# An encoder block on one core: separate banks for the first two block products of the feed-forward part, scratch tiles taken out, loads moved into the down projection, rotary tables computed earlier

## The chip, the cores and the metric

The kernel runs on one core of a Trainium2 chip. The metric is device time in microseconds (us) of one execution. Before the change three timed runs took 2662.81, 2665.69 and 2669.3 us, a median of 2665.69. The engines of the core are TensorE (PE, the matrix multiplies), VectorE (DVE), ScalarE (ACT), GpSimd (POOL) and SyncE (SP, which issues most of the DMAs, in order). PE writes into PSUM, which here is used as 8 banks of 128 partitions by 512 floats. Everything else is held in SBUF tiles.

## The reference

One sequence of S = 1024 tokens of width D = 1024 goes through DEPTH = 2 layers, all in f32:

```python
h = rms_norm(x, norm_mix_g[i])
z = h @ w_in[i]
q = apply_partial_rope(rms_norm(q, q_norm_g[i]), cos, sin)      # and k
o_attn = windowed_gqa_with_sink(q, k, v, sink[i])               # +-128 tokens
uv = gelu(z[..., GM_OFF:CONV_OFF]); o_gm = spatial_gating(uv, ...)
o_conv = conformer_conv(z[..., CONV_OFF:IN_COLS], ...)          # GLU, 31 taps, norm, swish
merged = concat(rms_norm(o_attn), rms_norm(o_gm), rms_norm(o_conv))
x = x + merged @ w_out[i]
hf = rms_norm(x, norm_ffn_g[i]) @ w_gate_up[i]                  # D_FF = 2816, gate and up
x = x + (silu(hf[..., :D_FF]) * hf[..., D_FF:]) @ w_down[i]
gate = sigmoid(rms_norm(x, ple_norm_g[i]) @ w_ple_gate[i])
x = x + (p[i] @ w_ple_proj[i]) * gate
```

## The kernel before

Activations are kept with features on the partitions and tokens along the row, in two halves of 512 tokens. Every product of two f32 operands is made of three matmuls in a reduced format: each operand is cut into a high part, which ACT copies out (`copy_h`, L122), and a low part, which DVE (sometimes POOL) gets by subtraction (`sub_l`, L125; for whole weight tiles L216). `step_mm` (L222 to L229) issues wh·hi (L224), wh·lo (L226) and wl·hi (L228) of 512 columns each.

A layer runs in stages. First come the input projection and the mixers. The 30 conv taps per channel block are DVE instructions (L493), issued piece by piece in the background of other work; `setup_gen`, another generator, computes the sine and cosine tables of the rotary step on DVE and ACT (L377 to L417). Then come the output projection (`wo_first`, `wo_second`), the feed-forward part, `down` and `ple`.

The feed-forward part multiplies by blocks, as Strassen's method does, with 7 block products per pair of output tiles where 8 would be the plain way. There are 11 pairs j. `first(j)` makes the two block products that need only the first token half: for gate (i = 0) and up (i = 1), 24 matmuls each, of which the first 12 (k below 4, one product) are read out by DVE as `s1` (L1131), sent to DRAM (`sum_d`), and the other 12 are then added on top in the same bank, so that PE waits at the middle of each unit until DVE has read. `token_forms(k)` makes the token-side sums for the other five products: per k 4 scalings (L1153), a difference `t1` (L1163), another on DVE (L1165), two on POOL, and five splits (L122 and L125). `rest(j)` makes the five other products: for i = 0 and then i = 1 it loads `s1` and two weight tiles `rw` (L1181), forms four weight sums on POOL (L1216, L1218, L1219, L1220; the first into a scratch tile `ws`), splits five weight blocks on ACT and DVE, runs five products of 12 matmuls, and adds and multiplies on DVE (L1208 and silu on ACT L1209 for i = 0; L1212 and L1213, through a scratch tile `cu`, for i = 1). The results go to DRAM (`act_d`, L1233 and L1234).

Order: firsts 0 to 4 run ahead, among the output projection; then the token forms; firsts 5 to 7; then rest 0, first 8, rest 1, first 9, rest 2, first 10, and rests 3 to 10 with nothing between them. After that come the transposes of `p` (L1267), the `ple` weights (L1275), and `down`: for each token half, 22 steps fi, each with a weight tile (`load_w`, L211 to L216), an activation tile `ac` (L1291) that is split, and 24 matmuls into all 8 banks.

Tiles come from pools: 38 `U` tiles of 128 by 1024, 6 `T` tiles of 128 by 512 (`s1`, `ws`, `cu`, `u2`, `g`, `ac`, `sg`, `sq`), 3 buffers each for `raw`, `wh`, `wl`, and PSUM banks `pa` (3), `pt` (4), `po` (1). An allocation waits until the tile that last had the buffer has been used for the last time. A scheduler orders each engine's instructions from the program text and the pools; the engines then run in that order.

Of the kernel before, what the change touches and what calls it, by code (L numbers as in the profile page):

```python
# [8 lines left out]
F32 = mybir.dt.float32  # L9
# [6 lines left out]
P = 128  # L16
# [55 lines left out]
def tile_encoder_trunk(ctx: ExitStack, tc: tile.TileContext, x, p, positions, norm_mix_g, w_in,  # L72
# [368 lines left out]
    for k in range(NK):  # L441
        if k + 1 < NK:
            x_in(k + 1)
        if k >= 3:
            next(setup, None)
# [15 lines left out]
    for layer in range(DEPTH):  # L461
# [656 lines left out]
        def first(j):  # L1118
# [3 lines left out]
            a = None  # L1122
            for i, off in enumerate((0, DFF)):
                wh, wl = load_w(rows_of(w_gate_up[layer], 0, NK, off + c0, P), (NK, P),
                                nc.gpsimd if ahead else None, nc.vector if ahead else None)
                b = BA()
                for k in range(NK):
                    step_mm(b, (wh[:, k, :], wl[:, k, :]), hl0[k], k == 0, k % HK == HK - 1, True)
                    if k == HK - 1:
                        s1 = T("s1")  # L1130
                        nc.vector.tensor_tensor(out=s1, in0=b, in1=bc, op=ALU.mult)  # L1131
                        nc.sync.dma_start(out=sum_d[j][i], in_=s1)
                    if k % 2 == 1:
# [39 lines left out]
        def rest(j):  # L1173

            ga, gb = U("ga"), U("gb")
            for i, off in enumerate((0, DFF)):
# [8 lines left out]
                sm = T("ws")  # L1185
                s3 = sm.rearrange("p (k m) -> p k m", k=HK)
# [19 lines left out]
                def out_of(dst, src, b):  # L1206
# [10 lines left out]
                w22 = None  # L1217
# [10 lines left out]
                out_of(gb[:, 512:1024], g, bc_)  # L1228
# [28 lines left out]

        pT = [[U("pT2", F32R) for _ in range(2)] for _ in range(2)]
        for hf in range(2):
            raw = wp.tile([P, 1024], F32, tag="raw", name=nm("pin"))  # L1260
            r3 = raw.rearrange("p (b m) -> p b m", b=4)
            nc.sync.dma_start(out=r3, in_=p[layer, 0, hf * 512:(hf + 1) * 512, :]
# [125 lines left out]
```

## Time and profile before

| | before |
|---|---|
| median of three timed runs | 2665.69 us |
| profiled execution, its own time | 2667.72 us |
| span of the trace | 2665.9 us |
| mean granted TensorE clock | 0.952 |
| PE busy | 2387.9 us (90%) |
| DVE / ACT / POOL busy | 1453.5 / 905.5 / 744.6 us |
| HBM read and written | 228.84 and 63.96 MB |

The span runs from the first to the last instruction; the profiled execution's own time is 1.8 us longer. [...] Idle time of PE plus the time lost at the lower clock is what an edit that leaves the arithmetic alone can win.

### The profile page before, as it was taken

What the parts mean: (1) busy time and instruction counts of PE and PEld (TensorE: products, weight loads), DVE (VectorE), ACT (ScalarE), POOL (GpSimd) and SP (SyncE); (2) the same over time, 40 slices, a digit from 0 to 9 for tenths busy, and PEclk for the clock granted to TensorE, in tenths of its full rate; (3) what the DMA queues carried; (4) which work ended last, traced back from release to release, by engine and by line L of the source; (5) the groups of instructions that cost most, each with busy time, mean ns of one, the idle gap of its engine ahead of it and who ended that gap; (6) DMA issues with size and microseconds to landing.
All of it is one profiled execution on the core that took longest, in us unless ns stands there. A gap on an engine that the chain in (4) does not pass through costs nothing. (4 is left out here: it accounts for less than half of the span.)

```text
span 2665.9 us, 30234 instructions
## 1 busy us (share of the span) xinstructions
PE 2387.9 (90%) x11404; PEld 1972.8 (74%) x11404; DVE 1453.5 (55%) x2241; ACT 905.5 (34%) x1610; POOL 744.6 (28%) x551
## 2 busy tenths in 40 slices
PE   8898889688988889899999898896898888898999
PEld 6897767567766668688789876675776666786887
DVE  6986674644544452525469567646444444526252
ACT  5246661312222241424323457412212222424142
POOL 5123345532332300103421233464323333001031
PEclk9999998899999989899999999898999999999999
DMA  6011324333333262523321031344333332625332
GB/s 205 24 52 56 119 84 161 118 124 113 131 103 103 87 217 95 198 95 107 96 71 37 33 111 64 126 150 123 123 111 99 103 103 87 241 95 197 95 99 67
DMA packets 243346, 294.78 MB, mean 111 GB/s; under 512 B 11348, under 2 KB 180912, under 8 KB 243200
## 3 DMA queue, kind: packets, MB, share of 16 engines
q1 hardware_dynamic: 236704, 283.16, 32.4%
q10 hardware_dynamic: 6016, 9.45, 1.1%
q8 instruction: 90, 1.47, 0.2%
q0 software_dynamic: 480, 0.24, 0.1%
q14 instruction: 56, 0.46, 0.1%
HBM read 228.84 MB, written 63.96 MB: 110 GB/s over the span
## 5 line engine op out<-in xcount | busy, mean ns | idle before, releaser
L216 DVE TENSOR_TENSOR wl<-raw,wh 128x1024 fp32r<-128x1024 f32 x172 | 218.9, 1273 | 337.5 <-ACT wh L122 327.7
L224 PE MATMUL pt<-tf,wh 128*128 128x512 f32 x792 | 326.5, 415 | 54.7 <-ACT wh L122 54.7
L122 ACT ACTIVATE wh<-raw 128x1024 fp32r<-128x1024 f32 x172 | 182.0, 1059 | 532.2 <-PE pt L226 376.9
L226 PE MATMUL pt<-tf,wh 128*128 128x512 f32 x792 | 323.3, 408 | 0.0
L224 PE MATMUL pa<-hl,wh 128*128 128x512 f32 x648 | 264.4, 409 | 62.9 <-DVE s L1131 52.9
L228 PE MATMUL pt<-tf,wl 128*128 128x512 f32 x792 | 315.4, 404 | 0.0
L224 PE MATMUL pa<-tf,wh 128*128 128x512 f32 x704 | 280.0, 400 | 19.5 <-ACT wh L122 19.5
L264 POOL TENSOR_TENSOR st<-st,sq 128x512 f32<-128x512 f32 x82 | 123.4, 1506 | 610.2 <-ACT sq L263 607.9
L228 PE MATMUL pa<-tf,wl 128*128 128x512 f32 x704 | 273.1, 394 | 9.2 <-DVE wl L125 9.2
L226 PE MATMUL pa<-tf,wh 128*128 128x512 f32 x704 | 277.0, 394 | 0.0
L228 PE MATMUL pa<-hl,wl 128*128 128x512 f32 x648 | 259.1, 404 | 4.5 <-POOL wl L216 3.3
L226 PE MATMUL pa<-hl,wh 128*128 128x512 f32 x648 | 262.1, 405 | 1.0 <-DVE hl L128 0.8
L224 PEld LDWEIGHTS pt<-tf,wh 128*128 128x128 f32 x792 | 159.4, 201 | 98.4 <-ACT wh L122 64.0
L1216 POOL TENSOR_TENSOR ws<-rw,rw 128x512 f32<-128x512 f32 x44 | 63.7, 1448 | 511.5 <-DVE cu L1212 337.6
L224 PEld LDWEIGHTS pa<-hl,wh 128*128 128x128 f32 x648 | 125.8, 194 | 99.6 <-DVE s L1131 59.3
L607 PE MATMUL pa<-wh,hl 128*128 128x256 f32 x640 | 181.1, 288 | 16.4 <-ACT zkv L620 11.7
L226 PEld LDWEIGHTS pt<-tf,wh 128*128 128x128 f32 x792 | 157.6, 199 | 33.9
L228 PEld LDWEIGHTS pt<-tf,wl 128*128 128x128 f32 x792 | 156.3, 197 | 34.2
L609 PE MATMUL pa<-wl,hl 128*128 128x256 f32 x640 | 181.6, 286 | 0.0
L610 PE MATMUL pa<-wh,hl 128*128 128x256 f32 x640 | 180.8, 286 | 0.0
L224 PEld LDWEIGHTS pa<-tf,wh 128*128 128x128 f32 x704 | 134.9, 192 | 55.7 <-ACT wh L122 28.8
L122 ACT ACTIVATE wh<-rw 128x512 fp32r<-128x512 f32 x176 | 102.6, 618 | 208.2 <-POOL rw L1218 172.8
(309 smaller groups left out, 4933.9 us busy)
## 6 DMA issues: line engine op xcount, KB each, us to landing
rw<-in_w_gate_up_dram SPq DMA_DIRECT2D x88, 512.0 KB, 6.0
raw<-in_w_down_dram SPq DMA_DIRECT2D x88, 512.0 KB, 3.6
raw<-in_w_gate_up_dram SPq DMA_DIRECT2D x44, 512.0 KB, 4.5
ac<-act SPq DMA_DIRECT2D x88, 256.0 KB, 5.0
raw<-in_w_ple_gate_dram SPq DMA_DIRECT2D x32, 512.0 KB, 4.1
raw<-in_w_in_dram SPq DMA_DIRECT2D x28, 512.0 KB, 3.8
raw<-in_w_out_dram SPq DMA_DIRECT2D x24, 512.0 KB, 3.7
sum<-s SPq DMA_DIRECT2D x44, 256.0 KB, 2.2
```

Of the source, the lines that this page charges most:

```text
L122: nc.scalar.activation(dst, src, AF.Copy, scale=scale)
L216: (eng or nc.vector).tensor_tensor(out=l, in0=raw, in1=f(h), op=ALU.subtract)
L224: nc.tensor.matmul(b, lhsT=wh, rhs=hl[:, 0:512], start=first, stop=False, skip_group_check=again)
L226: nc.tensor.matmul(b, lhsT=wh, rhs=hl[:, 512:1024], start=False, stop=False, skip_group_check=again)
L228: nc.tensor.matmul(b, lhsT=wl, rhs=hl[:, 0:512], start=False, stop=last, skip_group_check=again)
L264: (eng or nc.gpsimd).tensor_tensor(out=n.s, in0=n.s, in1=sq, op=ALU.add)
L607: nc.tensor.matmul(o, lhsT=x_[:, th], rhs=wh, start=(kc + k == 0), stop=False)
L609: nc.tensor.matmul(o, lhsT=x_[:, th], rhs=wl, start=False, stop=False)
L610: nc.tensor.matmul(o, lhsT=x_[:, tl], rhs=wh, start=False, stop=(kc == 1 and k == 3))
L1216: tt(out=s3, in0=a21, in1=a22, op=ALU.add)
```

## The change

The rotary tables' generator is advanced twice per step from k = 2 on, where it was once from k = 3. `first` loads the weights of both units up front and makes its products in separate banks (the three `pa` for the firsts ahead, `pa` and `pt` in turn for the others): the second bank is scaled in place and `s1` added, so DVE reads or writes a bank 7 times per first where it did 4 times, and the POOL multiply goes. In `rest` the weight sum is written into the left half of `ga`, and the up side adds in place in PSUM. The loads of `p` and of the `ple` weights go into `U` tiles, the `ac` tiles too; the `ple` weights are loaded at fi = 8, and X at fi = 12 of each half.

```diff
@@ -441,8 +441,9 @@
     for k in range(NK):
         if k + 1 < NK:
             x_in(k + 1)
-        if k >= 3:
-            next(setup, None)
+        if k >= 2:
+            for _ in range(2):
+                next(setup, None)
@@ -1119,27 +1120,30 @@
-            a = None
-            for i, off in enumerate((0, DFF)):
-                wh, wl = load_w(rows_of(w_gate_up[layer], 0, NK, off + c0, P), (NK, P),
-                                nc.gpsimd if ahead else None, nc.vector if ahead else None)
-                b = BA()
-                for k in range(NK):
-                    step_mm(b, (wh[:, k, :], wl[:, k, :]), hl0[k], k == 0, k % HK == HK - 1, True)
-                    if k == HK - 1:
-                        s1 = T("s1")
+            ws = [load_w(rows_of(w_gate_up[layer], 0, NK, off + c0, P), (NK, P),
+                         nc.gpsimd if ahead else None, nc.vector if ahead else None)
+                  for off in (0, DFF)]
+            a = T("sg")
+            for i, (wh, wl) in enumerate(ws):
+                bank = BA if ahead else BU
+                s1 = T("s1")
+                for h in range(2):
+                    b = bank()
+                    for k in range(h * HK, (h + 1) * HK):
+                        step_mm(b, (wh[:, k, :], wl[:, k, :]), hl0[k], k % HK == 0,
+                                k % HK == HK - 1)
+                        if k % 2 == 1:
+                            bg.tick()
+                    if h == 0:
                         nc.vector.tensor_tensor(out=s1, in0=b, in1=bc, op=ALU.mult)
                         nc.sync.dma_start(out=sum_d[j][i], in_=s1)
-                    if k % 2 == 1:
-                        bg.tick()
+                    else:
+                        nc.vector.tensor_tensor(out=b, in0=b, in1=bc, op=ALU.mult)
+                        nc.vector.tensor_tensor(out=b if i else a, in0=b, in1=s1, op=ALU.add)
                 if i == 0:
-                    a = T("sg")
-                    nc.vector.tensor_tensor(out=a, in0=b, in1=bc, op=ALU.mult)
                     nc.scalar.activation(a, a, AF.Silu)
-                    nc.gpsimd.tensor_tensor(out=a, in0=a, in1=bc, op=ALU.mult)
-                else:
-                    nc.vector.tensor_tensor(out=a, in0=b, in1=a, op=ALU.mult)
-                    nc.sync.dma_start(out=act_d[2 * j][:, HALF[0]], in_=a)
+            nc.vector.tensor_tensor(out=a, in0=b, in1=a, op=ALU.mult)
+            nc.sync.dma_start(out=act_d[2 * j][:, HALF[0]], in_=a)
@@ -1182,8 +1186,7 @@
-                sm = T("ws")
-                s3 = sm.rearrange("p (k m) -> p k m", k=HK)
+                s3 = ga[:, 0:512].rearrange("p (k m) -> p k m", k=HK)
@@ -1208,13 +1211,11 @@
                     else:
-                        c = T("cu")
-                        nc.vector.tensor_tensor(out=c, in0=b, in1=src, op=ALU.add)
-                        nc.vector.tensor_tensor(out=dst, in0=c, in1=dst, op=ALU.mult)
+                        nc.vector.tensor_tensor(out=b, in0=b, in1=src, op=ALU.add)
+                        nc.vector.tensor_tensor(out=dst, in0=b, in1=dst, op=ALU.mult)
@@ -1225,7 +1226,12 @@
-                out_of(gb[:, 512:1024], g, bc_)
+                if i == 0:
+                    out_of(gb[:, 512:1024], g, bc_)
+                else:
+                    nc.vector.tensor_tensor(out=g, in0=bc_, in1=g, op=ALU.add)
+                    nc.vector.tensor_tensor(out=gb[:, 512:1024], in0=g, in1=gb[:, 512:1024],
+                                            op=ALU.mult)
@@ -1255,44 +1261,50 @@
+        pin = [U("pin").rearrange("p (b m) -> p b m", b=4) for _ in range(2)]
+        for hf in range(2):
+            nc.sync.dma_start(out=pin[hf], in_=p[layer, 0, hf * 512:(hf + 1) * 512, :]
+                              .rearrange("(b q) m -> q b m", q=P))
...
-            raw = wp.tile([P, 1024], F32, tag="raw", name=nm("pin"))
...
-                ps = BT()
+                ps = BU()
...
-            raw = wp.tile([P, 1024], F32, tag="raw", name=nm("praw"))
...
+        def proj_weights():
+            for c in range(2):
+                raw = U("praw")
...
-            xps = [U("X").rearrange("p (m s) -> p m s", m=2) for _ in range(4)]
-            for mp in range(4):
-                nc.sync.dma_start(out=xps[mp], in_=xd[2 * mp:2 * mp + 2, :, HALF[hf]]
-                                  .rearrange("m p s -> p m s"))
             banks = [BO()] + [BA() for _ in range(3)] + [BT() for _ in range(4)]
             for fi in range(NF):
                 wh, wl = load_w(rows_of(w_down[layer], fi * P, 1, 0, D), (1, D))
-                t = T("ac")
+                t = U("ac")[:, 0:512]
...
+                if fi == 8 and hf == 0:
+                    proj_weights()
+                if fi == 12:
+                    xps = [U("X").rearrange("p (m s) -> p m s", m=2) for _ in range(4)]
+                    for mp in range(4):
+                        nc.sync.dma_start(out=xps[mp], in_=xd[2 * mp:2 * mp + 2, :, HALF[hf]]
+                                          .rearrange("m p s -> p m s"))
```

In the rows of the order below, numbers behind a name tell tiles apart.

The order of DVE near the end of the rotary tables in the first layer, before. L493 is a conv tap, `rt` the scratch of the tables; ACT's cosine follows L408:

```order
L383 SCALAR_TENSOR_TENSOR rt_462<-rt_462 128x64
L493 SCALAR_TENSOR_TENSOR acc_715<-glu_684,cols_190,acc_715 128x1019
L383 SCALAR_TENSOR_TENSOR rt_462<-rt_462 128x64
L493 SCALAR_TENSOR_TENSOR acc_715<-glu_684,cols_190,acc_715 128x1020
L383 SCALAR_TENSOR_TENSOR rt_462<-rt_462 128x64
L493 SCALAR_TENSOR_TENSOR acc_715<-glu_684,cols_190,acc_715 128x1021
L377 TENSOR_SCALAR rt_462<-rt_462 128x64
L493 SCALAR_TENSOR_TENSOR acc_715<-glu_684,cols_190,acc_715 128x1022
L408 TENSOR_SCALAR rt_462<-rt_462 128x64
```

And now, where a tap is L494:

```order
L494 SCALAR_TENSOR_TENSOR acc_715<-glu_684,cols_190,acc_715 128x1013
L383 SCALAR_TENSOR_TENSOR rt_388<-rt_388 128x64
L759 TENSOR_TENSOR rot_773<-sinf,qkg 128x8x8 x4
L216 TENSOR_TENSOR wl_1016<-raw_1014,wh_1015 128x1024
L125 TENSOR_TENSOR wst_763<-pt_766,wst_763 128x512
L494 SCALAR_TENSOR_TENSOR acc_715<-glu_684,cols_190,acc_715 128x1014
L377 TENSOR_SCALAR rt_388<-rt_388 128x64
L494 SCALAR_TENSOR_TENSOR acc_715<-glu_684,cols_190,acc_715 128x1015
L408 TENSOR_SCALAR rt_388<-rt_388 128x64
```

L408 stands behind the tap of length 1015 instead of the one of length 1022, that is 7 taps earlier.

The order of POOL in the rests without firsts, before. `ws` is the weight sum, `rw` are the loaded weights; four rows are one unit:

```order
L1216 TENSOR_TENSOR ws_7125<-rw_7121,rw_7122 128x512
L1218 TENSOR_TENSOR rw_7121<-rw_7121 128x4x128
L1219 TENSOR_TENSOR rw_7121<-ws_7125,rw_7121 128x4x128
L1220 TENSOR_TENSOR rw_7122<-rw_7122,rw_7121 128x4x128
L1216 TENSOR_TENSOR ws_7232<-rw_7228,rw_7229 128x512
```

And now, the sum being L1218 into `ga` and the other three L1219 to L1221:

```order
L1220 TENSOR_TENSOR rw_6917<-ga_6814,rw_6917 128x4x128
L1218 TENSOR_TENSOR ga_7016<-rw_7020,rw_7021 128x512
L1221 TENSOR_TENSOR rw_6918<-rw_6918,rw_6917 128x4x128
L1219 TENSOR_TENSOR rw_7020<-rw_7020 128x4x128
L1220 TENSOR_TENSOR rw_7020<-ga_7016,rw_7020 128x4x128
L1221 TENSOR_TENSOR rw_7021<-rw_7021,rw_7020 128x4x128
```

The first sum of the next rest's gate side (`ga_7016`) has moved ahead of the last one of this rest's up side.

The order of SP where `down` begins in the second layer, before. `act_118` and `act_117` are the last results of the feed-forward part, `raw` is a weight tile of `down`:

```order
L1181 DMA rw_16840<-in_w_gate_up_dram 128x4x256
L1275 DMA praw_16984<-in_w_ple_proj_dram 128x1024
L1234 DMA act_118<-gb_16736 128x1024
L1291 DMA ac_17012<-act_97 128x512
L211 DMA raw_17006<-in_w_down_dram 128x1024
L1291 DMA ac_17047<-act_98 128x512
L1291 DMA ac_17082<-act_99 128x512
L1233 DMA act_117<-ga_16735 128x512
```

And now, first a piece in the middle of the rests (`act_102` belongs to rest 2), then the one where `down` begins:

```order
L1185 DMA rw_15309<-in_w_gate_up_dram 128x4x256
L211 DMA raw_16999<-in_w_down_dram 128x1024
L1240 DMA act_102<-gb_15025 128x1024
L211 DMA raw_17034<-in_w_down_dram 128x1024
L1139 DMA sum_0_139<-s_2510_15239 128x512
```

```order
L1185 DMA rw_16822<-in_w_gate_up_dram 128x4x256
L1266 DMA pin_16920<-in_p_dram 128x4x256
L1266 DMA pin_16921<-in_p_dram 128x4x256
L1296 DMA ac_16970<-act_97 128x512
L211 DMA raw_17069<-in_w_down_dram 128x1024
L1296 DMA ac_17005<-act_98 128x512
L1296 DMA ac_17040<-act_99 128x512
L1240 DMA act_118<-gb_16719 128x1024
```

The first three weight tiles of `down` are loaded eight or nine rests earlier; the weight tile that now stands just before the last results is the fourth.

## Rows read from the trace of the kernel before

**Rows 1.** The page's busy line (engine, us, share of the span, instructions), then the view of PE's waits over the whole span: waiting tile and line, what it waited for, us in total, times, longest us.

```profile
PE 2387.9 (90%) x11404; PEld 1972.8 (74%) x11404; DVE 1453.5 (55%) x2241; ACT 905.5 (34%) x1610; POOL 744.6 (28%) x551
...
PE pt L224 <- ACT wh L122: 54.7, 22, 2.5
PE pa L224 <- DVE s L1131: 52.9, 14, 10.9
PE po L224 <- ACT tf L122: 31.1, 4, 8.8
PE pa L224 <- ACT wh L122: 19.5, 22, 0.9
PE pa L607 <- ACT zkv L620: 11.7, 1, 11.7
...
PE pa L228 <- DVE wl L125: 9.2, 14, 0.7
PE pt L511 <- DVE acc L493: 5.8, 1, 5.8
...
PE po L224 <- ACT wh L122: 4.5, 2, 2.3
```

**Rows 2.** The end of the rotary tables in the first layer. Timelines of ACT, DVE and PE (start us, us, engine, line, operation, out<-in, count, idle time before and its releaser), and between them two rows of the view by windows (stretch in us, its length, busy us of PE, PEld, DVE, ACT, POOL with counts, granted clock, DMA share, GB/s).

```profile
91.42 0.26 ACT L410 ACTIVATE cosf<-rt 128x64 f32<-128x64 f32 x1 [17.25 <-DVE rt L408]
...
91.20 0.19 DVE L408 TENSOR_SCALAR rt<-rt 128x64 f32<-128x64 f32 x1
...
92.00:96.00 4.00, 3.91 (x19) 3.91 (x20) 3.96 (x7) 0.76 (x3) 0.00 (x0) 0.53 0.00 0
122.00:192.00 70.00, 70.00 (x588) 70.00 (x587) 64.67 (x87) 29.43 (x58) 14.65 (x7) 1.00 0.15 50
...
189.78 2.57 DVE L493 SCALAR_TENSOR_TENSOR acc<-glu,cols,acc 128x1010 f32<-128x1010 f32 x2
...
195.61 1.58 PE L511 MATMUL pt<-ident,acc 128*128 128x128 f32 x13
```

**Rows 3.** The first of the firsts ahead in the second layer: PE's timeline, and the stretch around it by windows, columns as in rows 2.

```profile
1732.15 0.80 PE L224 MATMUL pa<-hl,wh 128*128 128x512 f32 x1 [1.47 <-DVE s L1131]
...
1738.65 0.50 PE L224 MATMUL pa<-hl,wh 128*128 128x512 f32 x1 [1.01 <-DVE sg L1137]
...
1720.00:1740.00 20.00, 14.20 (x42) 9.91 (x43) 17.53 (x27) 8.13 (x12) 7.22 (x6) 0.66 0.38 133
```

**Rows 4.** Token forms and firsts 5 to 7 in the second layer: the stretch by windows, columns as in rows 2, and rows of DVE's timeline in it.

```profile
1815.00:1870.00 55.00, 32.06 (x109) 23.91 (x108) 43.59 (x52) 17.13 (x30) 24.69 (x15) 0.78 0.29 91
...
1815.73 5.39 DVE L1153 SCALAR_TENSOR_TENSOR X<-X,cols,st 128x512 f32<-128x512 f32 x8 [2.46 <-ACT st L298]
...
1857.19 0.69 DVE L1131 TENSOR_TENSOR s<-pa,st 128x512 f32<-128x512 f32 x1 [2.50 <-PE pa L228]
...
1870.11 1.22 DVE L125 TENSOR_TENSOR wl<-rw,wh 128x512 fp32r<-128x512 f32 x1
```

**Rows 5.** PE's timeline at the middle of first 8's up unit in the second layer, and at the start of the rest behind it.

```profile
1911.56 0.50 PE L224 MATMUL pa<-hl,wh 128*128 128x512 f32 x1 [1.38 <-DVE s L1131]
...
1915.35 0.50 PE L224 MATMUL pa<-tf,wh 128*128 128x512 f32 x1 [0.78 <-ACT wh L122]
```

**Rows 6.** One rest without a first, in the first layer: timelines of PE, DVE and SP where its gate side begins, the time from issue to landing of the `rw` loads (L1181, 8 loads between 850 and 895 us), POOL's timeline for its up side, and the whole period by windows for PE alone (stretch, length, busy us of PE with count, granted clock, DMA share, GB/s).

```profile
855.86 0.50 PE L224 MATMUL pa<-tf,wh 128*128 128x512 f32 x1 [0.94 <-ACT wh L122]
...
854.96 0.69 DVE L1212 TENSOR_TENSOR cu<-pt,u 128x512 f32<-128x512 f32 x1 [0.96 <-PE pt L228]
855.69 1.36 DVE L1213 TENSOR_TENSOR ga<-cu,ga 128x512 f32<-128x512 f32 x1
...
857.08 0.32 SPq L1233 DMA_DIRECT2D act<-ga  x1
...
857.92 2.35 SPq L1181 DMA_DIRECT2D rw<-in_w_gate_up_dram  x4
...
DMA to landing us min/median/max: 4.1/6.0/7.6
...
864.61 1.30 POOL L1216 TENSOR_TENSOR ws<-rw,rw 128x512 f32<-128x512 f32 x1 [8.11 <-DVE g L1226]
...
867.35 1.29 POOL L1219 TENSOR_TENSOR rw<-ws,rw 128x512 f32<-128x512 f32 x1
...
855.00:888.80 33.80, 29.70 (x120) 0.95 0.31 102
```

**Rows 7.** Where `down` begins in the second layer: PE's and SP's timelines, and two stretches by windows, columns as in rows 2.

```profile
2282.64 0.80 PE L224 MATMUL po<-tf,wh 128*128 128x512 f32 x1 [6.85 <-ACT tf L122]
...
2275.83 0.33 SPq L211 DMA_DIRECT2D raw<-in_w_down_dram  x1
...
2282.68 1.97 SPq L211 DMA_DIRECT2D raw<-in_w_down_dram  x3
...
2282.00:2288.00 6.00, 5.36 (x14) 4.24 (x15) 4.27 (x6) 2.90 (x6) 0.00 (x0) 0.58 1.05 398
2294.00:2298.00 4.00, 4.00 (x12) 3.10 (x11) 3.83 (x5) 3.63 (x6) 0.00 (x0) 0.58 1.05 394
```

**Rows 8.** ACT's timeline in the middle of `down` (second layer), where the second token half begins.

```profile
2415.03 0.62 ACT L263 ACTIVATE sq<-X 128x512 f32<-128x512 f32 x1
2416.69 1.92 ACT L122 ACTIVATE tf<-ac 128x512 fp32r<-128x512 f32 x3 [1.05 <-DMA ac<-act]
```

More of the change, by code (lines that the diff above doesn't have):

```diff
@@ L1210, in out_of @@
                     else:
-                        c = T("cu")
-                        nc.vector.tensor_tensor(out=c, in0=b, in1=src, op=ALU.add)
-                        nc.vector.tensor_tensor(out=dst, in0=c, in1=dst, op=ALU.mult)
+                        nc.vector.tensor_tensor(out=b, in0=b, in1=src, op=ALU.add)
+                        nc.vector.tensor_tensor(out=dst, in0=b, in1=dst, op=ALU.mult)
                 bank = BT if i else BA
                 tt(out=s3, in0=a21, in1=a22, op=ALU.add)
-                w22 = None
                 tt(out=a21, in0=a11, in1=a21, op=ALU.subtract)
@@ L1255, in tile_encoder_trunk @@
                 first(AHEAD + 1 + BEHIND + j)
+        pin = [U("pin").rearrange("p (b m) -> p b m", b=4) for _ in range(2)]
+        for hf in range(2):
+            nc.sync.dma_start(out=pin[hf], in_=p[layer, 0, hf * 512:(hf + 1) * 512, :]
+                              .rearrange("(b q) m -> q b m", q=P))
         pT = [[U("pT2", F32R) for _ in range(2)] for _ in range(2)]
         for hf in range(2):
-            raw = wp.tile([P, 1024], F32, tag="raw", name=nm("pin"))
-            r3 = raw.rearrange("p (b m) -> p b m", b=4)
-            nc.sync.dma_start(out=r3, in_=p[layer, 0, hf * 512:(hf + 1) * 512, :]
-                              .rearrange("(b q) m -> q b m", q=P))
             for c in range(2):
-                ps = BT()
+                ps = BU()
                 for b in range(4):
-                    nc.tensor.transpose(ps[:, b * P:(b + 1) * P], r3[:, b, c * P:(c + 1) * P],
+                    nc.tensor.transpose(ps[:, b * P:(b + 1) * P], pin[hf][:, b, c * P:(c + 1) * P],
                                         ident)
@@ L1272, in tile_encoder_trunk @@
         pw = []
-        for c in range(2):
-            raw = wp.tile([P, 1024], F32, tag="raw", name=nm("praw"))
-            nc.sync.dma_start(out=raw, in_=w_ple_proj[layer, c * P:(c + 1) * P, :])
-            ph, pl = U("pwh", F32R), U("pwl", F32R)
-            copy_h(ph, raw)
-            sub_l(pl, raw, ph)
-            pw.append((ph, pl))
+        def proj_weights():
+            for c in range(2):
+                raw = U("praw")
+                nc.sync.dma_start(out=raw, in_=w_ple_proj[layer, c * P:(c + 1) * P, :])
+                ph, pl = U("pwh", F32R), U("pwl", F32R)
+                copy_h(ph, raw)
+                sub_l(pl, raw, ph)
+                pw.append((ph, pl))
         nx = [None, None]
         for hf in range(2):
-            xps = [U("X").rearrange("p (m s) -> p m s", m=2) for _ in range(4)]
-            for mp in range(4):
-                nc.sync.dma_start(out=xps[mp], in_=xd[2 * mp:2 * mp + 2, :, HALF[hf]]
-                                  .rearrange("m p s -> p m s"))
             banks = [BO()] + [BA() for _ in range(3)] + [BT() for _ in range(4)]
```

## The prediction

> **What bounds the kernel now.** I read the page's busy line first, then PE's waits, then the stretches in which they fall. PE is busy 2387.9 us of 2665.9 [rows 1], so TensorE bounds the kernel and 278 us of idle are all that an edit without fewer matmuls can win, apart from what PE loses at the lower clock. The reader is to see in the view of waits that few places make up the large lines, and that the diff touches nearly all of them: 22 waits of about 2.5 us for ACT's weight copy at the up side of a rest, 14 for `s1` (up to 10.9), 4 for a split in `down`, 22 short ones at the gate side of a rest, and one of 11.7 for ACT's `zkv` [rows 1]. Then the timelines tell for each what the engine named was itself waiting for. The sum below is made against the profiled execution's own 2667.7 us (span 2665.9 and 1.8 around it), which lies 2.0 over the median of 2665.7.
>
> **1. Rotary tables.** ACT's cosine stood 17.25 us for DVE's L408, which ended at 91.39, and `zkv` behind it released PE after 11.7 us [rows 1, 2]. In the new order L408 follows 7 taps fewer, at 1.28 us each (two took 2.57) [rows 2]: some 9 us earlier, so the wait shrinks to about 3, and the clock, 0.53 from 92 to 96 [rows 2], costs up to 1.9 less: 9 to 11 us won at this place. But the taps still have to be made. DVE is busy 64.67 us of the 70 from 122 to 192, its last tap ends at 192.35, and PE reads the sum at 195.61 [rows 2]. PE's lead over 3.3 us of slack turns into a wait there, as in the second layer, where PE stood 5.8 us for the taps [rows 1]; what DVE idled (5.3) is the rest that it can make up. I take 4 of bounds -2 and 11, near the slack.
>
> **2. Firsts ahead.** PE stands 1.47 us for `s1` and 1.01 for `sg`, and runs at a mean clock of 0.66 from 1720 to 1740 [rows 3]. The next 12 matmuls now have a bank of their own, and three banks cover the read-out, so both waits go, and the full clock should come about a microsecond sooner. 3.5 a layer, 7 in all, of bounds 0 and 10. More reads of PSUM come with it, 3 per first at 0.69 us [rows 4], on a DVE that is idle there once the token sums have not begun.
>
> **3. Token forms and firsts 5 to 7.** Waits for `s1` add up to 52.9 us [rows 1]; less 1.47 twice and 1.38 eight times (part 4) [rows 3, 5] this stage holds 38.9 of them. From 1815 to 1870 PE is busy 32.06 of 55 us, at a mean clock of 0.78 [rows 4]. It looks like a gain of 20 us a layer. But DVE is busy 43.59 of the 55 [rows 4], and from 1815.73 on its scalings and splits hold the waiting reads back. The separate banks let PE go on until its 7 banks are full; then it waits for the same DVE, which now has 9 reads more for three firsts, 9 x 0.69 = 6.2 us. 43.6 + 6.2 = 49.8 against 55 leaves 5.2 us if DVE never idles, more if part of the reads falls behind the first weights of rest 0, whose low part (L125) is made at 1870.11 [rows 4]. I take 6 a layer, 12 in all, of bounds 0 and 20.
>
> **4. Rests 0 to 3 with firsts between.** Per rest and first PE stands 1.38 us at the middle of the first and 0.78 at the gate side of the rest [rows 5]. The first of these goes with the separate banks, the second with `ws`, whose `T` buffer came free only when DVE had read an older one. 4 x 2.16 x 2 layers = 17.3; I take 17, of bounds 8 (only the first waits go, with something lost) and 18.
>
> **5. Rests alone, 7 a layer.** The period is 33.8 us at a clock of 0.95 [rows 6]. It holds 0.94 and 0.66 (the line of 9.2 over 14) at the gate side and 2.5 at the up side [rows 1, 6], and 1.7 (a twentieth) at the lower clock; the rest, 28.0 for 120 matmuls, makes 0.233 each and 2.8 per product. In the new order POOL makes the next gate side's first sum a unit early, so the gate side's waits go: 1.6 us. What is late next is the up side. Its weights are still loaded behind the store of `ga`: store at 857.08, `rw` from 857.92, POOL's first sum at 864.61 and the third ended at 868.64 [rows 6]. PE left the last product of the rest before at 855.86 - 0.94 = 854.92. Now 4 products (the first has been run ahead) end the gate side at 854.92 + 11.2 = 866.1, not at 870.7. The path through silu holds PE 2.5 us as before, to 868.6. The path through the loads: `ga` took 0.69 + 1.36 on DVE [rows 6] and in place should take 0.69 twice, so the loads, POOL and its third sum come 0.7 us earlier, at 868.0; a copy on ACT of 0.6 leads to 868.6 as well. So two paths meet, and any slip of the loads (4.1 to 7.6 us in this stretch, 6.0 in the middle [rows 6]) is paid in full; the 0.66 for the low part may come back here too. I take 1.0 a rest, 14 in all, of bounds -10 (a slip of 1.6 and a little more low clock in each) and 21 (1.5).
>
> [...]
>
> No row shows DVE writing into PSUM. From both sides: the nearest rows are 0.69 with a PSUM input and 1.36 beside POOL [rows 6]; I take 0.69.
>
> **6. Start of `down`.** SP issued the first weights of `down` at 2275.83, its next at 2282.68 behind the X loads, and PE stood 6.85 us, then about 2.3 [rows 1, 7]. With the first three weight tiles loaded during the rests, the fourth and `ac` on their way before the end, and X out of the queue, I see nothing late behind them. In both layers: the `po` lines hold 31.1 and 4.5 [rows 1]; two of the four long waits are those in the middle of `down`, 8.8 at most each [rows 1], which leaves at least 31.1 - 17.6 + 4.5 = 18. The clock was 0.58 over 6 and 4 us [rows 7]: 4.2 lost a layer, 8.4 in all. 26 of bounds 18 and 28.
>
> **7. Middle of `down`.** ACT ran the second norm's copies and squares until 2415.65, then waited 1.05 us for `ac` [rows 8]. Only that last us can go, since the copies stay ahead of the split: 2 in all, of bounds 0 and 4.
>
> **Sum.** 4 + 7 + 12 + 17 + 14 + 26 + 2 = 82. 2667.7 - 82 = 2585.7, and 2.0 less beside the median: 2584 us.
>
> **Rivals.**
> - DVE decides: the lead at the start is paid back whole, and the token stage gains nothing, since 9 more reads fill the time that PE wins (parts 1 and 3 at 0), and the loads keep the rests at 0.4 us each (6). For it: DVE's 43.59 of 55 and 64.67 of 70 us. Against it: DVE stood 2.50 us for PE at 1857 [rows 4], so it wasn't late all the way. 7 + 17 + 6 + 26 + 2 = 58: 2608. A chance of 0.25.
> - All is had: start 10, token stage 20, rests alone 21. For it: the largest waits have a cause that the diff removes. Against it: DVE's share again. 10 + 8 + 20 + 17 + 21 + 27 + 3 = 106: 2560. 0.15.
> - The loads into `down` don't do what they say: an early weight tile or an `ac` stands behind something unfinished in SP's queue, and the wait moves on to the fourth tile. For it: SP's order is strict. Against it: the three tiles are in place whole rests before. Without the 26: 56, 2610. 0.07.
> - Slower: the up side's loads become the bound of every rest. [...] With 4.5 us more and another 1.7 for 14 rests alone, and 2 for the 8 others, 103 us come in against 82 - 14 = 68 won: 2701. It decides from a slip of about 3 us in all rests. The longest landing, 7.6, is 1.6 over the middle. 0.05.
>
> **How the numbers follow.** The forecast has 0.45 and its own range is 2572 to 2598. What is left, 0.03, is no change, by several of these together. A difference under 0.2% (5 us) can't be told from no change here; faster by more than that 0.92, same 0.03, slower 0.05. The range goes from 2558, which takes in most of the case where all is had, to 2626, over the two at 2608 to 2610 and half of the unknown in part 5.
>
> **What would show it.** In the profile after: `zkv` at about 3 us, and a wait for taps in the first layer too (part 1); no wait for `s1` in the middle of a unit, and PE standing for DVE's reads of a bank in the token stage (3); in a rest alone no wait at the gate side, one of 2.5 to 3.2 at the up side, and a period near 32.8 (5); no wait over a us at the start of `down`, still about 7.5 in its middle (6, 7). The prediction fails if the up side's wait grows past 5 us, if DVE's in-place operations take more than 1 us where POOL is idle, or if the token stage ends no earlier and `down` still starts late.

## The result and the profile after

The changed kernel takes 2594.72 us (median of four, 2591.07 to 2603.97) beside 2664.47 of the kernel before: a ratio of 0.9741, 95% interval 0.9709 to 0.9772. That is faster, 11 us over the forecast of 2584 and inside its range. The profiled execution took 2591.07 (span 2589.2), 76.65 less than that of before. Two executions were far longer than the others of their kernel, 2966.47 us of banks_early (granted clock 0.741) and 5998.87 of the kernel before (1.0), and are left out of the times below.

The page's busy line, then PE's waits (tile and line, what it waited for, us in total, times, longest):

```profile
PE 2356.6 (91%) x11404; PEld 1965.9 (76%) x11404; DVE 1555.8 (60%) x2307; ACT 917.6 (35%) x1610; POOL 736.2 (28%) x529
...
PE pt L224 <- ACT wh L122: 62.1, 22, 4.0
PE pa L224 <- DVE sg L1142: 32.5, 4, 10.8
PE po L224 <- ACT tf L122: 14.6, 2, 7.3
...
PE pa L224 <- DVE s L1138: 10.4, 5, 7.3
...
PE pt L228 <- DVE wl L216: 6.8, 2, 6.4
PE pt L512 <- DVE acc L494: 5.8, 1, 5.8
```

Against [rows 1]: the line of `s1` is down from 52.9 to 10.4, that of `zkv` and that of the gate side are gone, `po` has 14.6 left of 31.1. But the up side's line grew from 54.7 to 62.1, and a new one has come: 32.5 us for L1142, which is the second of the two reads that the change adds to each second bank. The first matmuls of the stages in PE's timelines give the ledger (a `down` is counted up to its last matmul into `po`, the last row up to PE's last matmul):

| stage | before, us | after, us | difference |
|---|---|---|---|
| start to rest 0, layer 1 | 552.3 | 555.3 | +3.0 |
| rest 0 to `down`, layer 1 | 412.8 | 373.3 | -39.5 |
| `down`, layer 1 | 254.8 | 253.3 | -1.5 |
| end of `down` to rest 0 of layer 2 | 650.2 | 647.1 | -3.1 |
| rest 0 to `down`, layer 2 | 412.5 | 381.8 | -30.7 |
| `down`, layer 2 | 252.7 | 247.9 | -4.8 |
| what follows | 126.0 | 126.0 | 0.0 |

PE's windows over the rests, up to the last of them or to `down` (two layers before, two after; stretch, length, busy us with count, granted clock with 1.00 for full speed, DMA share, GB/s):

```profile
552.31:957.88 405.57, 360.59 (x1479) 0.95 0.32 104
1870.13:2275.52 405.39, 360.38 (x1479) 0.95 0.31 104
...
555.29:928.60 373.31, 341.22 (x1457) 0.97 0.35 117
1828.99:2210.70 381.71, 349.25 (x1481) 0.96 0.35 117
```

Layer 1 after has 24 matmuls fewer in this stretch than layer 2: two products of its last rest stand behind the first matmul of `down`. At 0.227 us each (seven that follow one another there start from 927.04 to 928.40) they are 5.4 us, so on equal work the second and third rows of the ledger read -34.1 and -6.9.

Parts 1 to 3 of the prediction lie in the first and the fourth row: 23 us were to come from there, and 0.1 came. The rests were to bring 17 + 14, and with them the first wait of `down` (13.8): 44.8, and 64.8 came. For `down` behind its first matmul the other 12.2 of part 6 and the 2 of part 7 were left, 14.2, and 11.7 came. So the total is nearly right by luck, by two errors of opposite sign.

The windows say more of the second error. PE's idle time in the rests fell by 25.4 us in all, less than the 31 of parts 4 and 5. Its busy time fell by 30.5; 5.4 of that are the 24 matmuls, and for the other 25 the same matmuls took less time, at a granted clock of 0.97 and 0.96 instead of 0.95. So the waits brought less than forecast, and what came on top came with the clock. Three places show what stands behind the rows.

**The firsts ahead, layer 2** (answers to [rows 3]). Timelines of DVE, POOL and PE:

```profile
1692.97 2.06 DVE L1157 SCALAR_TENSOR_TENSOR X<-X,cols,st 128x512 f32<-128x512 f32 x3
...
1695.56 3.49 DVE L1157 SCALAR_TENSOR_TENSOR X<-X,cols,st 128x512 f32<-128x512 f32 x2
1698.97 0.69 DVE L1141 TENSOR_TENSOR pa<-pa,st 128x512 f32<-128x512 f32 x1
1699.57 2.06 DVE L1157 SCALAR_TENSOR_TENSOR X<-X,cols,st 128x512 f32<-128x512 f32 x3
...
1702.15 0.69 DVE L1141 TENSOR_TENSOR pa<-pa,st 128x512 f32<-128x512 f32 x1
1702.76 0.67 DVE L1142 TENSOR_TENSOR sg<-pa,s 128x512 f32<-128x512 f32 x1
...
1695.77 2.73 POOL L216 TENSOR_TENSOR wl<-raw,wh 128x1024 fp32r<-128x1024 f32 x1 [8.44 <-DVE wh L215]
...
1703.48 0.79 PE L224 MATMUL pa<-hl,wh 128*128 128x512 f32 x1 [7.32 <-DVE sg L1142]
```

L1157 is the token scaling, formerly L1153, of token forms that come later in the program. DVE does them as they become ready, between the reads of the banks. So L1141 of the first unit's second bank stands until 1698.97, that of the second unit until 1702.15, and the bank is released by L1142 at 1702.76 + 0.67. With three `pa` banks and four products per first, PE has run into the unreleased bank: 7.32 us, where the old form waited 1.47 and 1.01. Two scalings took 3.49 us beside POOL's L216, three without it 2.06.

**A rest alone, layer 1** (answers to [rows 6]). SP, POOL, ACT and PE at the up side; then four periods by windows for PE alone (stretch, length, busy us with count, granted clock, DMA share, GB/s), two of rests alone and two of rests with firsts:

```profile
746.78 0.32 SPq L1239 DMA_DIRECT2D act<-ga  x1
...
747.67 2.05 SPq L1185 DMA_DIRECT2D rw<-in_w_gate_up_dram  x4
...
754.05 1.29 POOL L1218 TENSOR_TENSOR ga<-rw,rw 128x512 f32<-128x512 f32 x1 [18.52 <-DMA rw<-in_w_gate_up_dram]
...
756.76 1.26 POOL L1220 TENSOR_TENSOR rw<-ga,rw 128x512 f32<-128x512 f32 x1
...
756.01 0.63 ACT L1212 ACTIVATE ga<-ga 128x512 f32<-128x512 f32 x1 [2.09 <-DVE ga L1211]
...
758.06 0.63 ACT L122 ACTIVATE wh<-rw 128x512 fp32r<-128x512 f32 x1 [0.71 <-POOL rw L1220]
...
758.74 0.50 PE L224 MATMUL pt<-tf,wh 128*128 128x512 f32 x1 [3.49 <-ACT wh L122]
...
727.75:758.74 30.99, 27.50 (x120) 1.00 0.33 111
822.08:855.15 33.07, 29.07 (x121) 0.95 0.31 104
1845.26:1887.83 42.57, 40.09 (x168) 0.96 0.38 124
1887.83:1928.68 40.85, 38.37 (x168) 1.00 0.39 129
```

The gate side has no wait. At the up side the store of `ga` is issued at 746.78, the loads from 747.67, POOL begins when they have landed, its third sum ends at 758.02, the copy at 758.69, and PE starts at 758.74. Silu was done at 756.64, and the two copies behind it could have been by 757.7 (an estimate: PE stood from 755.25, and in ws_back, where the loads are in time, its wait is 2.48): the loads decide, by one us. The period is 30.99 at full clock; another in which the clock fell (0.95) has 33.07. Before, ten of the fourteen had 33.74 to 33.83 and 0.95; two had 32.2 and 1.00, two 35.4 and 0.90.

**The rotary tables and the middle of `down`** (answers to [rows 2, 8]). DVE's last tap and PE's first read of it in layer 1:

```profile
193.77 2.57 DVE L494 SCALAR_TENSOR_TENSOR acc<-glu,cols,acc 128x1010 f32<-128x1010 f32 x2
...
196.72 1.47 PE L512 MATMUL pt<-ident,acc 128*128 128x128 f32 x12
```

ACT and PE where the second token half of `down` begins, layer 2:

```profile
2336.71 0.61 ACT L263 ACTIVATE sq<-X 128x512 f32<-128x512 f32 x1
2337.23 0.61 ACT L122 ACTIVATE tf<-ac 128x512 fp32r<-128x512 f32 x1
...
2337.89 0.79 PE L224 MATMUL po<-tf,wh 128*128 128x512 f32 x1 [7.30 <-ACT tf L122]
```

The last tap ends at 196.34, 4.0 us later than before, and PE reads it at 196.72, 1.1 later, without a wait: the 5.8 us for `acc` in the list above is one wait, that of layer 2. In `down` PE still stands 7.30 us behind ACT's copies and squares.

### The profile page after: what moved, and what is told of

It is laid out like the page before. It is cut to its first block, busy times and chain, and to the rows that moved or that the text cites. A ratio compares the mean times of both kernels' runs of the same rounds, so it can differ in the third digit from the quotient of the medians.

```text
span 2589.2 us, 30142 instructions
## 1 busy us (share of the span) xinstructions
PE 2356.6 (91%) x11404; PEld 1965.9 (76%) x11404; DVE 1555.8 (60%) x2307; ACT 917.6 (35%) x1610; POOL 736.2 (28%) x529
## 3 DMA queue, kind: packets, MB, share of 16 engines
q1 hardware_dynamic: 236704, 283.16, 33.3%
q8 instruction: 90, 1.47, 0.2%
## 5 line engine op out<-in xcount | busy, mean ns | idle before, releaser
L216 DVE TENSOR_TENSOR wl<-raw,wh 128x1024 fp32r<-128x1024 f32 x172 | 217.7, 1266 | 292.9 <-ACT wh L122 285.5
L224 PE MATMUL pt<-tf,wh 128*128 128x512 f32 x792 | 320.1, 406 | 62.1 <-ACT wh L122 62.1
L226 PE MATMUL pt<-tf,wh 128*128 128x512 f32 x792 | 317.8, 401 | 0.0
L224 PE MATMUL pa<-hl,wh 128*128 128x512 f32 x564 | 232.9, 414 | 48.0 <-DVE sg L1142 32.5
L226 PE MATMUL pa<-tf,wh 128*128 128x512 f32 x704 | 275.3, 391 | 0.0
L224 PE MATMUL pa<-tf,wh 128*128 128x512 f32 x704 | 273.9, 391 | 0.0
L224 PEld LDWEIGHTS pt<-tf,wh 128*128 128x128 f32 x792 | 155.2, 196 | 103.4 <-ACT wh L122 71.0
L226 PE MATMUL pa<-hl,wh 128*128 128x512 f32 x564 | 229.2, 406 | 2.9 <-DVE hl L128 2.7
L228 PE MATMUL pa<-hl,wl 128*128 128x512 f32 x564 | 227.2, 403 | 0.0
L1218 POOL TENSOR_TENSOR ga<-rw,rw 128x512 f32<-128x512 f32 x44 | 63.8, 1451 | 514.3 <-DMA rw<-in_w_gate_up_dram 486.6
L125 DVE TENSOR_TENSOR wl<-rw,wh 128x512 fp32r<-128x512 f32 x176 | 186.1, 1071 | 30.1 <-ACT wh L122 28.1
L226 PEld LDWEIGHTS pt<-tf,wh 128*128 128x128 f32 x792 | 154.6, 195 | 32.4
L224 PEld LDWEIGHTS pa<-hl,wh 128*128 128x128 f32 x564 | 111.7, 198 | 77.5 <-DVE sg L1142 34.2
```

Of the source, the lines that this page charges most:

```text
L125: nc.vector.tensor_tensor(out=dst, in0=src, in1=f(h), op=ALU.subtract)
L216: (eng or nc.vector).tensor_tensor(out=l, in0=raw, in1=f(h), op=ALU.subtract)
L224: nc.tensor.matmul(b, lhsT=wh, rhs=hl[:, 0:512], start=first, stop=False, skip_group_check=again)
L226: nc.tensor.matmul(b, lhsT=wh, rhs=hl[:, 512:1024], start=False, stop=False, skip_group_check=again)
L228: nc.tensor.matmul(b, lhsT=wl, rhs=hl[:, 0:512], start=False, stop=last, skip_group_check=again)
L1218: tt(out=s3, in0=a21, in1=a22, op=ALU.add)
```

## The experiments

All times stand beside the kernel before in the same series. First the four parts of the diff alone, each put into the kernel before.

**only_a**: the tables' generator.

```diff
-        if k >= 3:
-            next(setup, None)
+        if k >= 2:
+            for _ in range(2):
+                next(setup, None)
```

> The kernel before with the rotary edit alone. Theory (DVE bounds the stage: the taps take back what PE wins): the 11.7 us wait for zkv goes, the work before the mixers' end is done no more than 1 to 4 us earlier, 2660 to 2664 us. Rival (the wait is lost time): 9 to 11 us won, 2653 to 2655.

Measured 2664.72, ratio 0.9988 (0.9971 to 1.0004). The wait for `zkv` is gone from its trace, and PE begins with the taps' sums at 196.50 where it was 195.61. It doesn't stand for the taps: by then it has begun 1288 matmuls, where it had 1211, a lead of some 8 us. The lead is lost behind the taps. From there to 300 us PE stands for 13.6 us instead of 8.1, for ACT's and DVE's `glu` and `mhl` above all, and the lower clock costs 8.5 instead of 5.1. The theory held in its number; that it is DVE which bounds the stretch is argued from the taps' later end and not shown by a run.

**only_b**: the firsts.

```diff
-                b = BA()
+                bank = BA if ahead else BU
+                for h in range(2):
+                    b = bank()
```

> The kernel before with the edit of the firsts alone. Theory (with three pa banks and two reads of each second bank queued behind the token scalings, the firsts ahead lose what the rest wins): a wait of about 7 us in the first of the firsts ahead in each layer, 10 lost there a layer, 3 to 8 won in the token stage, 5.5 in the rests with firsts: 2658 to 2670. Rival (that wait comes from the other edits, through the order): no such wait, 20 to 30 us won, 2635 to 2645.

Measured 2649.49, ratio 0.9943 (0.9925 to 0.9961): between the two, with the wait of the theory in it:

```profile
PE pa L224 <- DVE sg L1141: 43.6, 6, 7.8
```

(L1141 in this kernel is the second read.) The loss ahead is this part's own; what it wins in the rests was 7.2 and 7.5 us in the stretches from rest 0 to `down`, more than the 5.5 I had.

**only_c**: the rests.

```diff
-                sm = T("ws")
-                s3 = sm.rearrange("p (k m) -> p k m", k=HK)
+                s3 = ga[:, 0:512].rearrange("p (k m) -> p k m", k=HK)
...
-                        c = T("cu")
-                        nc.vector.tensor_tensor(out=c, in0=b, in1=src, op=ALU.add)
-                        nc.vector.tensor_tensor(out=dst, in0=c, in1=dst, op=ALU.mult)
+                        nc.vector.tensor_tensor(out=b, in0=b, in1=src, op=ALU.add)
+                        nc.vector.tensor_tensor(out=dst, in0=b, in1=dst, op=ALU.mult)
```

> The kernel before with the edit of the rests alone. Theory (the gate side's two waits hang on the T buffers of ws and cu and go without them, and the up side's wait stays under 4 us): periods of the rests alone 31 to 33 us, 1 to 2 won in each of 14 and 0.8 in 8 more: 2630 to 2645. Rival (the T buffers are short for the other edits' reasons too, so that this alone leaves the waits): 2660 or more.

Measured 2639.31, ratio 0.9898 (0.9878 to 0.9917).

```profile
PE pt L224 <- ACT wh L122: 77.9, 22, 5.0
PE pa L224 <- DVE s L1131: 40.8, 6, 9.9
```

The gate side's lines are gone, as the theory has it, but the up side's wait went up to 5.0 us, more than the 4 it allowed. And the eight waits of 1.38 us for `s1` in firsts 7 to 10 are gone too, without separate banks: in firsts 8 to 10 PE's order now has products of the rest in that place. So what I put down to the banks in part 4 either edit removes.

**only_d**: the loads (the hunks from `pin` on).

```diff
-                t = T("ac")
+                t = U("ac")[:, 0:512]
...
+                if fi == 12:
+                    xps = [U("X").rearrange("p (m s) -> p m s", m=2) for _ in range(4)]
```

> The kernel before with the edit of the loads alone. Theory (SP's order at the start of down is the whole cause): the waits of 6.9 and 2.3 us go, with 4 us of low clock, 11 to 13 a layer: 2638 to 2643. Rival (the early loads need the buffers that the other edits free): at most 8 us won, 2656 or more.

Measured 2632.79, ratio 0.9870 (0.9849 to 0.9892): 33 us, more than I expected and the largest part.

```profile
PE pa L224 <- ACT wh L122: 19.6, 22, 0.9
PE po L224 <- ACT tf L122: 14.6, 2, 7.3
```

The gate side's line is as before, the two waits at the start of `down` are gone. The four parts alone give 1.3 + 16.6 + 26.7 + 33.3 = 77.9 us by the medians, 8 more than the 69.8 of all together.

**x_moved**: the loads of X alone.

```diff
+                if fi == 12:
+                    xps = [U("X").rearrange("p (m s) -> p m s", m=2) for _ in range(4)]
+                    for mp in range(4):
+                        nc.sync.dma_start(out=xps[mp], in_=xd[2 * mp:2 * mp + 2, :, HALF[hf]]
+                                          .rearrange("m p s -> p m s"))
```

> The kernel before with the loads of X alone moved to fi = 12. Theory (the first wait at the start of down is that for down's first weights, issued late because the early places in the raw buffers went to p and to the ple weights; X only delays the next ones): the first wait stays at 6 to 7, the second (2.3) goes with its low clock, 8 us won: 2655 to 2660. Rival (X in SP's queue is the whole cause): 20 us or more won, under 2646.

Measured 2652.28, ratio 0.9942 (0.9923 to 0.9960), 18 us by the medians: more than the theory's 8, less than the rival's 20. PE's wait, SP and ACT where `down` begins in layer 2, and the stretch of layer 1's rests by windows (PE alone):

```profile
PE po L224 <- ACT wh L122: 12.6, 2, 6.4
...
2260.06 0.33 SPq L211 DMA_DIRECT2D raw<-in_w_down_dram  x1
...
2265.28 1.06 ACT L122 ACTIVATE wh<-raw 128x1024 fp32r<-128x1024 f32 x1 [2.22 <-DMA raw<-in_w_down_dram]
...
556.69:955.88 399.19, 354.19 (x1479) 0.97 0.32 106
```

The first wait stays (6.4), because `down`'s first weights are still issued at 2260.06; the second is gone. So the theory has the waits right. But the last row shows where much of the rest came from: the rests have the instructions and waits of before, which took 405.57 us at 0.95 there, and the clock was 0.97, 6.4 us less in this layer and 4.8 in the other. X is loaded behind this stretch, so I don't put that down to the edit, and it says how much of a difference between two kernels here may be the clock's: some 10 us.

Next, the firsts ahead in the changed kernel.

**old_ahead**: firsts 0 to 4 in the old form.

```diff
             c0 = 2 * j * P
+            if ahead:
+                for i, off in enumerate((0, DFF)):
+                    b = BA()
+                    for k in range(NK):
+                        step_mm(b, (wh[:, k, :], wl[:, k, :]), hl0[k], k == 0, k % HK == HK - 1, True)
...
+                return
```

> The changed kernel, the firsts ahead (0 to 4) alone back in their old form. Theory (the three pa banks fill and the second banks wait for two reads behind the token scalings on DVE): no wait of 7 us in the firsts ahead, s1 and sg waits of 1.5 and 1 instead, 8 to 12 us a layer won over the changed kernel: 2573 to 2581 beside 2664 of before. Rival (the loss comes with the order around the firsts, not with their banks): within 4 of the changed kernel, 2590 to 2598.

Measured 2576.74, ratio 0.9670 (0.9632 to 0.9707), 18 us under the changed kernel by the medians; in the traces rest 0 begins 9.0 us earlier in layer 1, and the stretch from `down` to rest 0 of layer 2 is 6.3 shorter. PE's waits for DVE in the firsts that are left:

```profile
PE pa L224 <- DVE sg L1165: 17.8, 2, 10.8
...
PE pa L224 <- DVE s L1161: 9.2, 3, 7.3
```

The two waits of 7.3 in the firsts ahead are gone (1.5 and 1.2 to 1.3 stand there again); those of 10.8 and 7.3 belong to the token stages.

**all_banks**: the firsts ahead on all seven banks.

```diff
-                bank = BA if ahead else BU
+                bank = BU
```

> The changed kernel with the firsts ahead taking pa and pt banks in turn, as the others do. Theory as in old_ahead: with seven banks PE doesn't come to the unread ones, so the waits of 7.3 go without another in their place: 2577 to 2585. Rival (DVE behind is what is short, and PE only stops later): a wait of 4 us or more stays in the firsts ahead, 2588 or more.

Measured 2577.30, ratio 0.9665 (0.9642 to 0.9688). As much as going back:

```profile
PE pa L224 <- DVE s L1138: 22.4, 4, 9.1
...
PE pa L224 <- DVE sg L1142: 7.6, 2, 6.9
```

The longest waits are all in the token stages now. The banks' number, not their separation, made the loss.

Then the up side's wait.

**early_loads**: both weight pairs of a rest loaded at its start.

```diff
-            for i, off in enumerate((0, DFF)):
-                s1 = T("s1")
...
+            for off in (0, DFF):
+                raw = [U("rw").rearrange("p (k m) -> p k m", k=HK) for _ in range(2)]
...
+            for i, raw in enumerate(raws):
+                s1 = T("s1")
+                nc.sync.dma_start(out=s1, in_=sum_d[j][i])
```

> The changed kernel with both weight pairs of a rest loaded at its start, so that the up side's don't stand behind the store of ga of the rest before. Theory (the loads decide the up side's wait, and with them ACT's order, in which the up side's first copies then stand ahead of silu): the line of 62 us for wh at the up side falls below 15, periods of the rests alone 28 to 29 us: 2535 to 2550. Rival (silu decides): the wait stays at 2.5 each, 55 in all, 2585 to 2592.

Measured 2516.67, ratio 0.9445 (0.9426 to 0.9463): 78 us under the changed kernel, better than the theory's numbers. ACT in a rest alone (layer 1), and one period:

```profile
705.34 0.63 ACT L122 ACTIVATE wh<-rw 128x512 fp32r<-128x512 f32 x1 [3.60 <-POOL rw L1222]
708.56 1.15 ACT L122 ACTIVATE wh<-rw 128x512 fp32r<-128x512 f32 x2 [2.59 <-PE pa L228]
...
714.19 0.63 ACT L122 ACTIVATE wh<-ga 128x512 fp32r<-128x512 f32 x1 [1.65 <-PE pa L226]
714.73 0.62 ACT L122 ACTIVATE wh<-rw 128x512 fp32r<-128x512 f32 x1
...
719.84 0.63 ACT L1215 ACTIVATE ga<-ga 128x512 f32<-128x512 f32 x1 [0.24 <-DVE ga L1214]
...
702.85:730.05 27.20, 27.20 (x122) 1.00 0.39 126
```

All five copies of the up side (705.34, two from 708.56 on, 714.19 and 714.73) now stand ahead of silu of `ga` (719.84), PE has no wait in the rests alone, and the period is 27.20 us at full clock. SP still issues a rest's four loads right behind a store of `ga` (at 709.02, the loads from 709.98), but that store is now a rest earlier for the up side, whose first sum POOL makes at 729.33. Both the loads' wait and silu's have gone: with the weights loaded earlier, the scheduler itself orders ACT so. Which of the two brought how much, the run doesn't tell.

**ws_back**: the weight sum in a `T` tile again.

```diff
-                s3 = ga[:, 0:512].rearrange("p (k m) -> p k m", k=HK)
+                s3 = T("ws").rearrange("p (k m) -> p k m", k=HK)
```

> The changed kernel with the weight sum back in a scratch T tile. Theory (the T buffer of ws is what held POOL's first sum, so that the gate side's weights came late): POOL's order is the old one again, the gate side's waits of 0.9 and 0.7 come back in the rests alone, periods near 33.5, 15 to 25 us lost against the changed kernel: 2609 to 2620 beside 2666 of before. Rival (cu and ac were the users that kept the T buffers short): no gate side waits, 2592 to 2598.

Measured 2582.27, ratio 0.9672 (0.9657 to 0.9687), 12 us faster than the changed kernel. The theory falls; the rival is right about the waits, but its time was 2592 to 2598.

```profile
PE pt L224 <- ACT wh L122: 52.8, 22, 2.5
...
752.44 1.29 POOL L1218 TENSOR_TENSOR ws<-rw,rw 128x512 f32<-128x512 f32 x1 [19.57 <-DMA rw<-in_w_gate_up_dram]
```

The gate side's waits stay away, so with `cu` and `ac` out of the pool `ws` was no longer short. And 20 of the 22 waits at the up side are 2.48 or 2.49, the other two shorter, 9.3 us less in all than in the changed kernel. In this kernel PE's order has all five products of the gate side behind the up side (60 `pa` matmuls in a row from 743.18 on); in the changed one the first is run ahead (14 of them from 736.05 on, then 24 of the up side), and the cover for the loads is a product, 2.7 us, shorter. POOL's third sum ends at 756.47 here, before PE's wait begins at 756.94. Silu of `ga` ends at 758.33 by an estimate (1.39 behind the start of the wait, as in the changed kernel), and silu decides.

**cu_back**: the up side through scratch tiles.

```diff
-                        nc.vector.tensor_tensor(out=b, in0=b, in1=src, op=ALU.add)
-                        nc.vector.tensor_tensor(out=dst, in0=b, in1=dst, op=ALU.mult)
+                        c = T("cu")
+                        nc.vector.tensor_tensor(out=c, in0=b, in1=src, op=ALU.add)
+                        nc.vector.tensor_tensor(out=dst, in0=c, in1=dst, op=ALU.mult)
```

> The changed kernel with the up side's sums back in scratch T tiles (no writing in place in PSUM). Theory (a product with both inputs in SBUF stretches beside POOL, the store of ga and the loads behind it come 0.7 us later, and the loads decide the up side's wait): that wait's line grows from 62 to 70 to 80 us: 2602 to 2614. Rival (the store's 0.7 us is slack): within 4 of the changed kernel.

Measured 2589.75, ratio 0.9702 (0.9686 to 0.9717), 5 us under the changed kernel, where the rival allowed 4 either way and the theory wanted a loss.

```profile
PE pt L224 <- ACT wh L122: 60.6, 22, 3.7
...
L1216 DVE TENSOR_TENSOR ga<-cu,ga 128x512 f32<-128x512 f32 x22 | 15.1, 684 | 0.0
```

The `ga` product takes 0.684 us with both inputs in SBUF, so its 1.36 of before [rows 6] didn't go because of PSUM, and the wait didn't grow. That one ran beside POOL's L1220 (855.22 to 856.50); in the changed kernel POOL stands from 735.53 to 754.05, and the product, at 746.07, takes 0.69. I put the difference down to POOL's order. In place or not is the same here.

Last, what beats both.

**banks_early**: all_banks and early_loads.

```diff
-                bank = BA if ahead else BU
+                bank = BU
...
+                raws.append(raw)
+            for i, raw in enumerate(raws):
```

> All_banks and early_loads together. If the two are independent the gains add: 2520 to 2540. If the early loads take buffers that the firsts need, less than the better of the two.

Measured 2490.63 (median of three), ratio 0.9346 (0.9316 to 0.9377): the gains add (17 and 78 singly, 104 together).

**halves_joined**: that, and the first three steps of `down`'s second half prepared ahead of the norm.

```diff
+            if hf == 0:
+                ready = [down_in(1, fi) for fi in range(3)]
             nx[hf] = Norm()
```

> Banks_early with the weights and activations of the first three steps of down's second token half loaded and split ahead of the norm of the first half. Theory (the wait of 7.3 in the middle of down is ACT's order alone: 16 copies and squares ahead of the split): that wait and the 2.3 behind it fall below 2 together, 8 to 11 us a layer with the low clock: 2468 to 2478 beside 2493 of banks_early. Rival (DVE, which adds X to eight banks one after the other, holds PE then): a wait of 4 us or more for X or hl in its place, 2484 or more.

Measured 2466.70, ratio 0.9261 (0.9241 to 0.9280), the fastest. Two of the largest waits left:

```profile
PE pa L224 <- DVE s L1138: 23.9, 5, 5.9
...
PE po L224 <- ACT tf L122: 8.6, 2, 4.3
```

No wait is left in the middle of `down` in either layer (the 8.6 is at its start, where early_loads already has 4.3 a layer): ACT's order was the whole of it, and DVE's adding of X held nothing up.

## Why the prediction came out as it did

1. Rotary tables: the wait went whole, where about 3 was to stay, and all of it was paid back. The term of 4 should have been 0 (only_a: 1.3, not told from nothing). The place was wrong: PE doesn't wait for the taps in layer 1, though they end 4.0 us later. It comes there with more matmuls begun (1287 in the changed kernel, where it had 1211), and loses the lead behind them.
2. Firsts ahead: wrong in sign. The step that failed is "three banks cover the read-out". A first has four products; each second bank needs two reads, and "a DVE that is idle there" was busy with token scalings (three in 2.06 us, but two in 3.49 beside POOL's subtraction). [rows 3] could have said so: DVE was busy 17.53 of the 20 us from 1720 on. 7 won were expected; old_ahead says that the form cost some 18 (15.3 in the two rows of the ledger), and all_banks that seven banks do cover the read-out.
3. Token forms: the mechanism was right. PE now stands for the release of banks (7.0 and 10.8 in layer 1; 1.9 and 7.3 in layer 2) instead of `s1` within a bank, and in layer 2 once 6.4 us for the low part of a weight tile (L216). Taking the loss of point 2 out of the ledger (old_ahead has 546.3 and 640.8 in the two rows) leaves 6.0 and 9.4 in the two layers, 15.4 for points 1 and 3 together, near the 4 + 12 that I took.
4. Rests with firsts: 45.2 before, 41.7 after as means of six periods, 3.4 us instead of 2.16. The waits went as said (4.64 to 2.48); the rest is the clock, 0.96 or 0.97 in each period before and 1.00 in half of those after. I had left the low clock in every period.
5. Rests alone: 31.7 and 32.0 a period in the two layers, 1.8 to 2.1 won instead of 1.0. PE's idle time gave 0.7 of it (4.1 a period before, 3.4 after), less than I took; the rest came with the clock. That two paths meet at the up side was right; the loads are the later, by 0.4 to 1.5 us. The 0.7 us from the product in place was right in size and wrong in cause: cu_back has it too. No row showed DVE writing into PSUM, and the 0.69 that I took holds: the sums in place took 0.699 us in the changed kernel, the products with an input in PSUM 0.683 and 0.685, and the one with both inputs in SBUF 0.691 (0.684 and 0.689 in cu_back).
6. Start of `down`: right. The waits are gone in the trace; its first waits and the `down` rows of the ledger give 13.8 + 11.7 = 25.5 beside the 28 of parts 6 and 7 together. only_d with 33 us alone gave more, and x_moved shows that the clock has its part in such a number.
7. Middle of `down`: 7.3 and 2.6 where there were 8.5 and 1.5 in layer 2, so nothing, not 2.

Of the rivals, the one where DVE decides was the nearest in time. Of its three conditions one came true, the lead at the start that is paid back whole; the token stage did gain, and so did the rests. The slower one, in which the loads set each rest, began: the up side's wait grew to 4.0, and to 5.0 in only_c. What it would have cost shows in early_loads from the other side. No run shows its second 1.7 us of low clock a rest as a rule: of the twelve periods of rests alone in the changed kernel that end in waits of 2.85 to 4.00 us, two lost that much (0.90, waits of 3.59 and 3.61), and five stood at 1.00, with waits up to 3.81.

## What to carry to other kernels

Before you call a buffer's wait won, count the buffers against the products between two releases, and look at what else stands in the queue of the engine that releases them. The up side's loads, issued behind the store of the last result and needed soon after, were late by the whole chain (store at 746.78, PE at 758.74). Issuing them a rest earlier was worth 78 us on top of the change, more than the 70 of the change itself, and the scheduler reordered the work behind it as well; the kernel before was not tried with it. And where a period holds several waits and a lower clock, ask what the clock does once one wait is left.

## What the hardware showed that I had not expected

In these traces the granted clock followed more than the length of one wait. In the changed kernel periods with a wait of 3.49 or 3.81 us stayed at 1.00, those with 3.59 and 3.61 stood at 0.90, and with waits of 2.48 (ws_back, layer 1) neighbouring periods of rests alone alternated between 0.99 and 0.95. And the same rests, with the same waits, ran at 0.95 in the kernel before and at 0.97 in x_moved, 11 us apart in two layers. DVE's scalings with both inputs in SBUF took 0.69 us each without POOL (three in 2.06) and 1.75 on average beside one POOL subtraction of 2.73 (two in 3.49).
